# The bonus of a RWKV-7 head in two fp32r products in place of one fp32 product

## The chip, the cores and the metric

One Trainium2 chip, one of its cores. The metric is the time of one execution of the whole kernel on the device, in microseconds (us), the median of three runs. Engines: PE (TensorE, matrix products), DVE (VectorE), ACT (ScalarE), POOL (GpSimd), SP (SyncE, which issues most of the DMAs). fp32r is a second four-byte type of PE's inputs; the kernel splits an fp32 value into its copy in fp32r, the high part, and what that leaves, the low part.

## The reference

One layer of a hybrid decoder for 1024 prompt tokens and 8 x 4 sample tokens. One projection feeds RWKV-7 time mixing (8 heads of 64) and, beside it, dilated window attention (3 groups of 4 heads of 128); both are gated, projected, merged, and normalised. The change touches one term of the time mixing, the bonus:

```python
def rwkv_mix(zs, z_gate, wkv0, w0, w_w2, a0, w_a2, k_k, k_a, r_k, lnx_g, lnx_b):
    ...
    S_fin, o = lax.scan(step, wkv0.astype(F32), xs)
    ...
    o = ((o - mu) * lax.rsqrt(var + GN_EPS)).reshape(B, T, R_WIDTH) * lnx_g.astype(F32) + lnx_b.astype(F32)
    bonus = (jnp.sum(r * k * r_k.astype(F32), -1, keepdims=True) * v).reshape(B, T, R_WIDTH)
    y = (o + bonus) * jax.nn.silu(z_gate.astype(F32))
```

The sum runs over the 64 values of a head, for each token.

## The kernel before, in words

The activations stand transposed in SBUF (columns on the 128 partitions, tokens along the free axis), split once into a high and a low part, both fp32r. A weight block comes in by DMA (`load_w`, L159 to L163: `wraw`), ACT copies its high part to fp32r (`whi`, L162), DVE subtracts it for the low part (`wlo`, L163), and `mm3` (L172) makes three fp32r products of each pair, high by high, low by high and high by low, over chunks of 352 tokens into the PSUM banks `pj`. These products fill most of PE's time.

The time mixing runs from some 30 to 620 us. It is cut into eight units: head pair j (0 to 3, two heads on 128 partitions) times half hf (0 or 1, 512 tokens). A unit goes through four generators. `unit` prepares: norms of the keys, decays (L330), the scaled operands `KR` and `BK` (L346 to L356), the product of r, k and r_k in `rk` (L358), the two halves of the products `AT` (PE L370, DVE's masked copy L377), then the bonus (L389: `rk` by the matrix of ones per head `bones`, a part of the constants `cst`; L390 multiplies by v), transposed values `W` (PE L397, ACT L400), transposed keys `BT` (PE L407, ACT L408). `inverse` solves the triangular systems on DVE (L441, L444), `scan` (L463 to L511) carries the state over the chunks, `norm` (L544 to L557) normalises and adds the bonus.

The generators are advanced by one planner that keeps a clock of costs: each `yield (cost, due)` adds its cost to the clock and says when the stream may go on; between them the planner puts pieces of the projection's products. What comes out is PE's order, which is fixed by hand (a manual schedule for PE alone); the order on the other engines is made by the framework's scheduler. The bonus announces its cost at L391, `yield (0.85, D_G)`.

Tiles with the tag "t" are 128x512 fp32 in a ring of six buffers; the tag "g" is two PSUM banks, "sc" two, "pj" four. After the time mixing come the sample rows, the attention of the heads, the two branch products and the output stage (L1378, fp32r products of 512 columns).

Of the kernel before, what the change touches and what calls it, by code (L numbers as in the profile page):

```python
# [11 lines left out]
F32 = mybir.dt.float32  # L12
F32R = mybir.dt.float32r
I32 = mybir.dt.int32
AF = mybir.ActivationFunctionType
ALU = mybir.AluOpType
AX = mybir.AxisListType

P = 128
# [12 lines left out]
D_PN, D_KR, D_AT, D_G, D_W, D_INV, D_UP = 0.65, 1.81, 7.0, 0.2, 2.09, 0.9, 14.4  # L32
# [51 lines left out]
def tile_layer(ctx: ExitStack, tc: tile.TileContext, A: dict, O: list):  # L84
    nc = tc.nc
    V, S, G, T, SP = nc.vector, nc.scalar, nc.gpsimd, nc.tensor, nc.sync
# [10 lines left out]
    def mk(pool, shape, tag, bufs=None, dt=F32):  # L97
        uid[0] += 1
        return pool.tile(list(shape), dt, tag=tag, name=f"{tag}_{uid[0]}", bufs=bufs)

    def ps(tag, cols=512, parts=P):
        pool = pspool if tag == "pj" else pp[0]
        return mk(pool, [parts, cols], tag, {"pj": PJ, "sc": 2, "g": 6 - PJ, "s": 1, "t": 2, "o": 1}[tag])
# [12 lines left out]
    rp = rw_stack.enter_context(tc.tile_pool(name="rp", bufs=1))  # L116
# [3 lines left out]
    bones, rmask = cst[:, 0:128], cst[:, 384:896]  # L120
# [117 lines left out]
    V.tensor_scalar(der[:, HB : HB + 24], prm[:, BG : BG + 24], 0.5, None, ALU.mult)  # L238
    V.tensor_scalar(der[:, KA2 : KA2 + 4], prm[:, KA : KA + 4], -0.5, 1.0, ALU.mult, ALU.add)
    V.tensor_scalar(der[:, KAH : KAH + 4], prm[:, KA : KA + 4], 0.5, None, ALU.mult)  # L240
    lhi = mk(rp, [P, 512], "lhi", dt=F32R)
    llo = mk(rp, [P, 512], "llo", dt=F32R)
    S.activation(lhi[:], lraw, AF.Copy)
# [61 lines left out]
    def unit(j, hf, Mr, Mk, Mv, st, out):  # L305
# [50 lines left out]
        V.tensor_tensor(BK[:, :, 0:4:3, :], c2p(k2), c2p(Ei), ALU.mult)  # L356
        rk = t_()
        V.scalar_tensor_tensor(rk[:], Mr[:, sl], prm[:, RK + j : RK + j + 1], k2[:], ALU.mult, ALU.mult)  # L358
        done["prep"] += 1
        yield (0.45, D_AT)  # L360

# [2 lines left out]
        for h in range(2):  # L364
            pA = [ps("g") for e in range(2)]
            for q in range(4):
                c = 4 * h + q
                for e in range(2):
# [5 lines left out]
                        start=True, stop=True,  # L374
# [11 lines left out]
            yield None  # L386
        bon = t_("bon", 2)
        pb = ps("g")
        T.matmul(pb[:], bones, rk[:], start=True, stop=True)  # L389
        V.tensor_tensor(bon[:], pb[:], Mv[:, sl], ALU.mult)  # L390
        yield (0.85, D_G)  # L391


        W = mk(rp, [P, 8, P], "W", 2)
# [17 lines left out]
        for c2 in range(4):  # L412
            for e in range(2):
                for p in range(2):
# [3 lines left out]
                        start=True, stop=True,  # L418
# [244 lines left out]
    def units():  # L663
        for u in range(8):
            j, hf = u // 2, u % 2
            while j not in pairs:
                yield None
            M, st = pairs[j]
            yield from unit(j, hf, M[0], M[1], M[2], st, ready)
            done["unit"] += 1  # L670
        yield from sample_rows()
# [688 lines left out]
    for i in range(8):  # L1360
# [9 lines left out]
        for c, (c0, c1) in enumerate(zip(parts, parts[1:])):  # L1370
            cs = slice(c0, c1)
            pb = ps("pj", c1 - c0)
# [51 lines left out]
```

## Time and profile before

| | |
|---|---|
| median of three runs | 1381.0 us (1380.83 to 1381.04) |
| profiled execution | 1381.54 us |
| its span | 1379.8 us |
| mean granted clock of PE | 0.996 |
| PE busy | 1344.1 us, 97% |
| DVE busy | 804.0 us, 58% |
| ACT busy | 467.2 us, 34% |
| POOL busy | 67.2 us, 5% |

The profile is one execution as the hardware recorded it. Busy times are shares of the whole span; an engine that waits is idle, and the wait is put down to what released it. The ends of matrix products are modelled, so the time that PE spends on one is best read from the start of one to the start of the next.

### The profile page before, as it was taken

The page shows a single profiled execution, that of the slowest core. Times are in us where ns is not written, and L with a number is a line of the kernel's source. Part 1 is how long each engine was busy: PE and PEld are TensorE (multiplying, and loading weights), DVE is VectorE, ACT ScalarE, POOL GpSimd, SP SyncE. Part 2 cuts the span into 40 slices and gives each one's busy share as a digit, 9 for nine tenths or more (in the row PEclk, how much of TensorE's full clock was granted, in tenths as well). Part 3 has the DMA queues.
Part 4 walks back from the last instruction along what each step waited for, and adds up shares of the span by engine and source line. Part 5 has one row for each costly group of instructions (what it writes and reads, how often), then busy time and mean ns, then how long its engine had stood idle before and what let it go on. Part 6 is the DMA issues. An engine that isn't in the chain of part 4 may idle for free.

```text
span 1379.8 us, 25342 instructions
## 1 busy us (share of the span) xinstructions
PE 1344.1 (97%) x9809; PEld 1245.0 (90%) x9809; DVE 804.0 (58%) x2203; ACT 467.2 (34%) x1089; POOL 67.2 (5%) x82
## 2 busy tenths in 40 slices
PE   7999999999999999999999999999999999899997
PEld 7998998898988889999999999999999998799786
DVE  4358767677867757441555275437542845665565
ACT  4333434444344444431332333233323234132211
POOL 0000000000000000000100000000000000015100
PEclk9999999999999999999999999999999999999999
DMA  6112222412322242336645355635554556795221
GB/s 216 55 47 73 58 82 72 110 37 75 88 59 75 74 110 79 91 94 123 136 106 132 84 141 115 131 93 140 114 123 115 133 122 153 230 287 170 82 103 68
DMA packets 340270, 151.62 MB, mean 110 GB/s; under 512 B 188928, under 2 KB 329622, under 8 KB 339894
## 3 DMA queue, kind: packets, MB, share of 16 engines
q1 hardware_dynamic: 241270, 129.68, 34.6%
q10 hardware_dynamic: 98880, 20.32, 7.4%
q8 instruction: 77, 1.26, 0.4%
q14 instruction: 43, 0.35, 0.1%
HBM read 110.68 MB, written 38.97 MB: 108 GB/s over the span
## 4 chain that ended last, share of the span: by engine, by line
PE 74%; DVE 14%; DMA 7%; issue 2%; ACT 2%; SPq 1%; DVEq 0%; ACTq 0%
PE pj L172 52%; PE pj L1378 7%; DVE tm L441 2%; DVE X L444 2%; PE o L932 2%; DMA cb<-cd 2%; PE s L895 2%; DMA wraw<-in_w_in_dram 1%; DVE wlo L163 1%; DVE o L1178 1%; PE t L915 1%; PE sc L503 1%; PE s L1014 1%; PE g L370 1%; DVE AT L377 1%
## 5 line engine op out<-in xcount | busy, mean ns | idle before, releaser
L172 PE MATMUL pj<-xhi,whi 128*128 128x352 f32 x1848 | 398.7, 337 | 5.0 <-ACT xhi L1245 3.0
L172 PE MATMUL pj<-xlo,whi 128*128 128x352 f32 x1848 | 382.8, 328 | 0.0
L172 PE MATMUL pj<-xhi,wlo 128*128 128x352 f32 x1848 | 381.9, 328 | 0.4 <-DVE wlo L163 0.4
L172 PEld LDWEIGHTS pj<-xhi,whi 128*128 128x128 f32 x1848 | 302.9, 189 | 21.7 <-issue 10.5
L172 PEld LDWEIGHTS pj<-xhi,wlo 128*128 128x128 f32 x1848 | 307.6, 189 | 3.6 <-issue 1.2
L172 PEld LDWEIGHTS pj<-xlo,whi 128*128 128x128 f32 x1848 | 307.9, 189 | 2.5 <-issue 0.4
L163 DVE TENSOR_TENSOR wlo<-wraw,whi 128x512 fp32r<-128x512 f32 x162 | 113.4, 701 | 84.0 <-ACT whi L162 83.3
L162 ACT ACTIVATE whi<-wraw 128x512 fp32r<-128x512 f32 x162 | 100.6, 625 | 146.6 <-PE pj L172 89.0
L905 ACT ACTIVATE Sm<-Sm,nm 128x128 f32<-128x128 f32 (+1 forms) x96 | 42.4, 442 | 102.7 <-DVE nm L902 102.7
L511 DVE SCALAR_TENSOR_TENSOR st<-sc,E,SD 64x64 f32<-64x64 f32 x128 | 36.2, 283 | 47.7 <-PE sc L508 46.2
L441 DVE TENSOR_TENSOR tm<-Y,X 128x60 f32<-128x60 f32 (+24 forms) x248 | 52.6, 212 | 6.3
L444 DVE TENSOR_TENSOR X<-X,tm 128x60 f32<-128x60 f32 (+24 forms) x248 | 52.0, 210 | 6.4
L1378 PE MATMUL pj<-wl,mh 128*128 128x512 f32 (+1 forms) x136 | 52.0, 382 | 0.0
L897 DVE CUSTOM_DVE_ANT_0 Sm<-s,cst 128x128 f32<-128x128 f32 (+1 forms) x96 | 29.2, 346 | 39.0 <-PE s L895 38.3
L494 ACT ACTIVATE SD<-st,E 128x128 f32<-128x128 f32 x64 | 25.6, 400 | 58.5 <-DVE st L511 58.5
L758 POOL TENSOR_TENSOR kvp<-vv,kv 128x512 f32<-128x512 f32 x16 | 19.7, 1233 | 514.3 <-DVE Ss L766 387.0
L932 PE MATMUL o<-PT,Vt 128*128 128x128 f32 x280 | 38.7, 276 | 0.8 <-ACT PT L919 0.8
L895 PE MATMUL s<-k,q 128*128 128x128 f32 (+1 forms) x192 | 37.8, 326 | 1.7 <-DVE ml L897 1.6
L820 ACT ACTIVATE k<-pj 128x352 f32<-128x352 f32 (+1 forms) x36 | 16.2, 454 | 67.5 <-PE pj L172 60.9
L932 PEld LDWEIGHTS o<-PT,Vt 128*128 128x128 f32 x280 | 36.4, 191 | 1.5 <-ACT PT L919 1.1
L503 PEld LDWEIGHTS sc<-R,AT 64*64 64x64 f32 x256 | 19.7, 134 | 18.4 <-DVE R L498 7.9
L299 ACT ACTIVATE zt<-pj,der 128x352 f32<-128x352 f32 x48 | 26.4, 551 | 27.9 <-PE pj L172 26.7
(314 smaller groups left out, 1719.1 us busy)
## 6 DMA issues: line engine op xcount, KB each, us to landing
wraw<-in_w_in_dram SPq DMA_DIRECT2D x146, 256.0 KB
gd<-zt SPq DMA_DIRECT2D x48, 176.0 KB
gt<-gd SPq DMA_DIRECT2D x48, 176.0 KB
vs<-bt ACTq DMA_DIRECT2D x48, 128.0 KB
kc<-in_cache_kv_g_dram SPq DMA_DIRECT2D x48, 128.0 KB
Vt<-vs ACTq DMA_DIRECT2D x12, 512.0 KB
cb<-cd SPq DMA_DIRECT2D x12, 512.0 KB
zd<-zt SPq DMA_DIRECT2D x24, 176.0 KB
```

Of the source, the lines that this page charges most:

```text
L162: S.activation(hi[:], raw[:], AF.Copy)
L163: V.tensor_tensor(lo[:], raw[:], hi.bitcast(F32)[:], ALU.subtract)
L172: T.matmul(out, w[wi][:, n % 4, :], x[:, n % 4, :], start=first and n == 0, stop=last and n == 11)
L441: V.tensor_tensor(tm, Y[:, r : r + 1, r + 1 : 32].to_broadcast([P, m, n]), X[:, 0:m, r : r + 1].to_broadcast([P, m, n]), ALU.mult)
L444: V.tensor_tensor(X[:, 0:m, r + 1 : 32], X[:, 0:m, r + 1 : 32], tm, ALU.subtract)
L503: T.matmul(pu[u, 64 * e : 64 * e + 64], AT[u, e, c, u], R[u, 64 * e : 64 * e + 64], start=True, stop=True)
L511: V.scalar_tensor_tensor(S1[d, d], pS[d, d], E[d, c, 64:65], SD[d, d], ALU.mult, ALU.add)
L895: T.matmul(r, qT[:, i * P : (i + 1) * P], kT[:, keys[i][0] * P : keys[i][0] * P + n], start=True, stop=True)
L897: V.tensor_tensor_reduce(out=Sm[:, i, 0:n], in0=r, in1=m3 if g == 2 else m12[:, 256 - n : 256], scale=1.0, scalar=NEG, op0=ALU.add, op1=AL ...
L905: S.activation(Sm[:, i, 0:n], Sm[:, i, 0:n], AF.Exp, scale=SCALE, bias=nm[:, x : x + 1], accum_out=ml[:, g, 1, i : i + 1])
L932: T.matmul(po[:, (i % 4) * P : (i % 4 + 1) * P], st["Vt"][:, kb_, :], PT[:, n * P : (n + 1) * P], start=m == 0, stop=m == len(keys[i]) - 1,)
L1378: T.matmul(pb[:], a[:, k], wk, start=x == 0, stop=x == len(prods) - 1)
```

## The change

Three places. After the derived parameters, the matrix of ones is copied once into a fp32r tile, `bones_r`. In `unit`, behind `rk`, ACT copies `rk` to fp32r (`rkh`) and POOL subtracts that from `rk` (`rkl`, fp32r too); both come from the ring "t". The bonus then is two fp32r products that add up in the same bank, and it announces a cost of 0.47 in place of 0.85.

```diff
     V.tensor_scalar(der[:, KAH : KAH + 4], prm[:, KA : KA + 4], 0.5, None, ALU.mult)
+    bones_r = mk(rp, [P, P], "bones_r", dt=F32R)
+    V.tensor_copy(bones_r[:], bones)
     lhi = mk(rp, [P, 512], "lhi", dt=F32R)
...
         rk = t_()
         V.scalar_tensor_tensor(rk[:], Mr[:, sl], prm[:, RK + j : RK + j + 1], k2[:], ALU.mult, ALU.mult)
+        rkh, rkl = (mk(rp, [P, 512], "t", 6, dt=F32R) for _ in range(2))
+        S.activation(rkh[:], rk[:], AF.Copy)
+        G.tensor_tensor(rkl[:], rk[:], rkh.bitcast(F32)[:], ALU.subtract)
         done["prep"] += 1
         yield (0.45, D_AT)
...
         pb = ps("g")
-        T.matmul(pb[:], bones, rk[:], start=True, stop=True)
+        T.matmul(pb[:], bones_r[:], rkh[:], start=True, stop=False)
+        T.matmul(pb[:], bones_r[:], rkl[:], start=False, stop=True)
         V.tensor_tensor(bon[:], pb[:], Mv[:, sl], ALU.mult)
-        yield (0.85, D_G)
+        yield (0.47, D_G)
```

PE's order around the bonus of unit 4, before (L389 is the bonus, L172 the weight products, L496, L503 and L508 steps of the scan):

```order
L548 MATMUL g_3985<-ident_69,Ot_3216 128x128 x4
L389 MATMUL g_3997<-t_3842,cst_76 128x512
L496 MATMUL sc_4003<-st_114_794,KR_3043 128x128
L397 MATMUL g_4009<-ident_69,m_3442 128x128 x4
L172 MATMUL pj_3887<-xlo_9_87,whi_3891 128x352 x4
L503 MATMUL sc_4020<-R_4005,AT_3131 64x64 x2
L407 MATMUL g_4025<-ident_69,BK_3839 128x128 x4
```

And with the change (t_3866 is the high part, t_3867 the low one; line numbers from there on are higher by 2 to 7):

```order
L554 MATMUL g_4011<-ident_69,Ot_3238 128x128 x4
L394 MATMUL g_4023<-t_3866,bones_r_358 128x512
L395 MATMUL g_4023<-t_3867,bones_r_358 128x512
L502 MATMUL sc_4030<-st_115_796,KR_3060 128x128
L403 MATMUL g_4036<-ident_69,m_3464 128x128 x4
L172 MATMUL pj_3913<-xlo_9_87,whi_3917 128x352 x4
L509 MATMUL sc_4047<-R_4032,AT_3152 64x64 x2
L413 MATMUL g_4052<-ident_69,BK_3861 128x128 x4
```

The pair stands where the one product stood, here as in the units 0 to 5; what the planner puts behind the bonus changes only from unit 6 on.

ACT's order at the same place, before (L550 is the scaled copy of `norm`, L400 the copies of the transposed values, L499 the scan's output):

```order
L483 ACTIVATE AT_3131<-sc_3966 32x8x32 x2
L550 ACTIVATE Ot_3216<-g_3985,prm_339 128x512
L400 ACTIVATE W_4008<-g_4009 64x4x128
L499 ACTIVATE Ot_4000<-sc_4003 64x128
L400 ACTIVATE W_4008<-g_4009 64x4x128
L504 ACTIVATE W_3224<-sc_4020 64x128
```

With the change:

```order
L489 ACTIVATE AT_3152<-sc_3992 32x8x32 x2
L556 ACTIVATE Ot_3238<-g_4011,prm_339 128x512
L505 ACTIVATE Ot_4027<-sc_4030 64x128
L406 ACTIVATE W_4035<-g_4036 64x4x128 x2
L510 ACTIVATE W_3246<-sc_4047 64x128
```

The copy of the scan's output has moved ahead of the first of the two copies of the values.

DVE's order ahead of the masked copies of unit 7, before (L152 to L154 are the Newton steps of `norm`'s inverse root, L544 its scaling, L358 makes `rk`):

```order
L358 SCALAR_TENSOR_TENSOR t_6174<-m_4637,prm_339,t_6169 128x512
L152 SCALAR_TENSOR_TENSOR nt_6122<-nt_6122,v_1195_6119 128x8
L153 TENSOR_TENSOR nt_6122<-nt_6122 128x8
L154 SCALAR_TENSOR_TENSOR nt_6122<-nt_6122 128x8
L544 TENSOR_TENSOR Ot_5536<-Ot_5536,nt_6122 128x512
L377 TENSOR_TENSOR AT_6236<-g_6237,cst_76 128x512
```

With the change:

```order
L360 SCALAR_TENSOR_TENSOR t_6215<-m_4668,prm_339,t_6210 128x512
L152 SCALAR_TENSOR_TENSOR nt_6163<-nt_6163,v_1210_6160 128x8
L153 TENSOR_TENSOR nt_6163<-nt_6163 128x8
L154 SCALAR_TENSOR_TENSOR nt_6163<-nt_6163 128x8
L550 TENSOR_TENSOR Ot_5572<-Ot_5572,nt_6163 128x512
L163 TENSOR_TENSOR wlo_6683<-wraw_6680,whi_6682 128x512
L382 TENSOR_TENSOR AT_6284<-g_6285,cst_76 128x512
```

A subtraction of a weight split has come in ahead of the first masked copy.

## Rows read from the trace of the kernel before

**Rows 1.** The page: busy time, share of the span and instructions of PE.

```profile
PE 1344.1 (97%) x9809; PEld 1245.0 (90%) x9809; DVE 804.0 (58%) x2203; ACT 467.2 (34%) x1089; POOL 67.2 (5%) x82
```

**Rows 2.** Stretches: us, busy PE, PEld, DVE, ACT, POOL, clock, DMA share, GB/s.

```profile
30.00:620.00 590.00, 579.10 (x4659) 535.39 (x4658) 388.38 (x1311) 237.59 (x537) 6.88 (x20) 1.00 0.27 76
119.90:123.80 3.90, 2.87 (x26) 2.24 (x25) 3.66 (x15) 0.62 (x2) 0.00 (x0) 1.00 0.60 172
303.00:306.40 3.40, 3.40 (x14) 2.90 (x14) 3.30 (x16) 1.81 (x4) 0.00 (x0) 0.50 0.42 100
```

**Rows 3.** PE's waits from 30 to 640 us: total us, times, longest.

```profile
PE g L370 <- DVE AT L377: 2.7, 8, 1.0
PE g L407 <- ACT W L400: 2.6, 6, 0.4
```

**Rows 4.** Timeline of PE at unit 2's bonus: start, duration in us.

```profile
206.56 1.12 PE L389 MATMUL g<-t,cst 128*128 128x512 f32 x2
207.52 0.27 PE L496 MATMUL sc<-st,KR 128*128 128x128 f32 x1
```

**Rows 5.** Timeline of PE in the output stage, fp32r products of 512 columns.

```profile
1303.99 0.47 PE L1378 MATMUL pj<-xhi,mh 128*128 128x512 f32 x1
1304.30 0.39 PE L1378 MATMUL pj<-xhi,ml 128*128 128x512 f32 x1
1304.54 0.40 PE L1378 MATMUL pj<-wl,mh 128*128 128x512 f32 x1
```

**Rows 6.** The page's groups: ACT's copy to fp32r (busy us, mean ns).

```profile
L162 ACT ACTIVATE whi<-wraw 128x512 fp32r<-128x512 f32 x162 | 100.6, 625 | 146.6 <-PE pj L172 89.0
```

**Rows 7.** POOL's instructions of line 758: shortest, median, longest ns.

```profile
L758 POOL TENSOR_TENSOR kvp<-vv,kv x16: 1042/1044/1550, 656.0 to 1061.6; 128x512 f32<-128x512 f32 x16
```

**Rows 8.** Timelines of DVE and PE in unit 7: `rk` and its bonus.

```profile
499.03 0.74 DVE L358 SCALAR_TENSOR_TENSOR t<-m,prm,t 128x512 f32<-128x512 f32 x1
505.38 0.70 PE L389 MATMUL g<-t,cst 128*128 128x512 f32 x1
```

**Rows 9.** Timeline of DVE at the start; in brackets idle time and its releaser.

```profile
28.21 0.27 DVE L232 COPY shT<-g 128x104 f32<-128x104 f32 x1 [2.23 <-PE g L231]
```

**Rows 10.** Timelines of POOL and DVE in a later stage.

```profile
821.70 1.42 POOL L758 TENSOR_TENSOR kvp<-vv,kv 128x512 f32<-128x512 f32 x1 [30.74 <-DVE Ss L766]
822.14 1.53 DVE L767 TENSOR_TENSOR rtm<-Ss,kv 128x512 f32<-128x512 f32 x1
863.23 0.69 DVE L767 TENSOR_TENSOR rtm<-Ss,kv 128x512 f32<-128x512 f32 x1
```

**Rows 11.** Timelines of DVE and PE in unit 1.

```profile
119.97 0.69 DVE L163 TENSOR_TENSOR wlo<-wraw,whi 128x512 fp32r<-128x512 f32 x1
123.08 0.68 DVE L377 TENSOR_TENSOR AT<-g,cst 128x512 f32<-128x512 f32 x1
123.82 0.37 PE L370 MATMUL g<-KR,BK 64*128 64x128 f32 x1 [1.05 <-DVE AT L377]
```

**Rows 12.** Timelines of DVE and PE in unit 4.

```profile
320.83 0.15 DVE L154 SCALAR_TENSOR_TENSOR nt<-nt 128x8 f32<-128x8 f32 x1
322.12 0.44 DVE L463 STREAM_TRANSPOSE T<-AT 32x256 f32<-32x256 f32 x1
322.62 0.24 PE L467 MATMUL sc<-T,AT 32*32 32x32 f32 x2 [0.28 <-DVE T L463]
```

**Rows 13.** Timeline of DVE in units 2 and 3.

```profile
202.88 0.69 DVE L377 TENSOR_TENSOR AT<-g,cst 128x512 f32<-128x512 f32 x1 [0.79 <-PE g L370]
261.29 0.69 DVE L163 TENSOR_TENSOR wlo<-wraw,whi 128x512 fp32r<-128x512 f32 x1 [0.91 <-ACT whi L162]
```

**Rows 14.** Timelines of DVE and PE in units 6 and 7.

```profile
442.33 0.69 DVE L377 TENSOR_TENSOR AT<-g,cst 128x512 f32<-128x512 f32 x1 [0.53 <-PE g L370]
443.08 0.37 PE L370 MATMUL g<-KR,BK 64*128 64x128 f32 x1 [0.15 <-DVE AT L377]
502.46 0.37 PE L370 MATMUL g<-KR,BK 64*128 64x128 f32 x1 [0.15 <-DVE AT L377]
```

## The prediction

> **What bounds the kernel now.** I read the page first, then the stretch in which the change lies, then PE's waits there, then single instructions. The page gives PE busy for 97% of the span [rows 1]. The eight units (head pair 0 to 3 times half 0 or 1; I number them 0 to 7) run between 30 and 620 us, and there PE is busy for 579.10 of 590.00 us while DVE is busy for 388.38, ACT for 237.59 and POOL for 6.88 [rows 2]. So some 11 us of idle time is all that PE has there: time taken off PE is time off the span, unless PE then waits for something, and time that another engine loses costs nothing until PE waits for it. The places where PE waits are therefore the ones to read: the first products of a unit's second half (L370) wait 2.7 us in eight times, up to 1.0, for DVE's masked copy L377, and L407 waits 2.6 us in six for ACT's L400 [rows 3]. The first is where the change can hurt, since its new POOL instruction is put just ahead of it.
>
> One bound for the whole text: what a measurement of this kernel can tell from no change is about 0.2%, 2.76 us.
>
> **The product of the bonus (removed and added).** The fp32 product of 512 columns is two MATMULs; in unit 2 it starts at 206.56 and the next product starts at 207.52 [rows 4], so it holds PE for 0.96 us. For two fp32r products of 512 columns the nearest rows are those of the output stage: one starts at 1303.99 behind another kind of product, the next at 1304.30, the one behind both at 1304.54 [rows 5]. That is 0.55 us for two, the first dearer than the second (0.31 and 0.24); if both cost the second's, 0.48. The other end is that the pair is no cheaper than what it replaces, 0.96. I take 0.55, for the bonus too follows another kind of product. Saved: 0.96 - 0.55 = 0.41 a unit, **8 x 0.41 = 3.3 us** (ends: 0, and 8 x 0.48 = 3.8).
>
> The Trainium skill (TensorE: Matmul & The Clock Gate, section "Back-to-back issue gap") gives a lone product of N columns at full clock N/2.4 + 2.5 ns, 216 ns for 512 columns. By it the pair is an estimated 0.43 us, the saving 4.2 us and the sum below 0.9 us lower; the trace's 0.24 is a tenth above it, and the sum stays with the rows.
>
> What follows the bonus on PE starts sooner by 0.41. Behind it L407 waits 0.43 for ACT in six units [rows 3]; were that wait to grow by what PE gained, 6 x 0.41 = 2.5 of the 3.3 would go. I take it as kept: the order on ACT now has the copy of the scan's output ahead of both copies L400 in the middle units, where it stood between them, and so the second L400 starts sooner. Both ends (0 and 2.5) go to the range.
>
> **The high part on ACT (added).** Eight copies 128x512 to fp32r; the same form takes 625 ns [rows 6]. 8 x 0.63 = 5.0 us on an engine that idles 352 of the 590 us [rows 2]. I cost it at nothing; what hides it is that idle time, and if it stood in the way of the next unit's weight split on ACT, that would be late by 0.63 at most.
>
> **The low part on POOL (added), by itself.** A subtraction of 128x512 on POOL takes 1.04 us when alone, and up to 1.55 [rows 7]. POOL is idle otherwise. Is the bonus late for it? In unit 7, the tightest, the instruction that makes its input starts at 499.03 and takes 0.74, and the bonus starts at 505.38 [rows 8]: 5.6 us for a chain of 0.63 + 1.04 to 1.55, which fits in all units. At nothing, then, as to its own result. The change's conversion of the matrix of ones is one DVE copy at the start, ahead of L232, where DVE stands idle for 2.23 us [rows 9]: nothing.
>
> **What the low part does to DVE.** This is the term that decides. In the later stage, where POOL runs the same form beside DVE, a DVE instruction with two operands in SBUF that starts 0.44 us after POOL's at 821.70 takes 1.53 us; the same line takes 0.69 where POOL is quiet [rows 10]. POOL's own took 1.42 against 1.04. 821.70 + 1.42 = 823.12, and 822.14 + 1.53 = 823.67: DVE's ends 0.55 us after POOL's, so it did next to nothing until POOL had finished. So the two engines exclude each other, and POOL's 1.04 us is taken out of DVE's time wherever DVE has instructions with two SBUF operands to run. The low part starts about 0.7 us after its input is made, just in the stretch before L377.
>
> How much of 1.04 reaches PE is read from each unit's stretch:
> - Unit 1: DVE is busy for 3.66 of the 3.90 us from 119.90 [rows 2], from a weight split at 119.97 on, without a gap, to L377 at 123.08, for which PE's L370 already waits 1.05 [rows 11]. Everything DVE loses there, PE loses: between 0.7 (one instruction there, of 0.5, has an operand in PSUM and can run on if it comes to stand beside POOL's) and 1.04; I take 0.87.
> - Unit 4: the delay falls between L154 at 320.83 and the transposition L463 at 322.12, for which PE's L467 already waits 0.28 [rows 12]: 1.0.
> - Units 2 and 3: ahead of what follows DVE idles 0.79 and 0.91 us [rows 13], which takes up most of 1.04; 0.25 and 0.13 are left on DVE, about 0.12 each reaches PE. Units 0 and 5 are like them, 0.1 each.
> - Unit 6: idle 0.53 before L377, and PE waits 0.15 behind it already [rows 14]: 1.04 - 0.53 = 0.5, I take 0.4.
> - Unit 7: PE waits 0.15 [rows 14] and DVE's order now has a weight split (about 0.69, the form of [rows 11]) ahead of L377, behind POOL's instruction: 0.65.
>
> Sum of the losses: 0.87 + 1.0 + 2 x 0.12 + 2 x 0.1 + 0.4 + 0.65 = **3.4 us** (ends: 0, if the delays all fall into idle time, and 8 x 1.04 = 8.3, if none does).
>
> **The order.** The lower cost that the bonus announces leaves PE's order as it is through unit 5; from unit 6 on one group of four weight products stands earlier, and the rest follows shifted by one group. Nothing waits for that but what is named at unit 7. At nothing.
>
> **The sum.** -3.3 + 3.4 = +0.1 us on the profiled execution's 1381.54 (span 1379.8 and 1.7 around it), 1381.6. The runs' median, 1381.0, is 0.54 below that execution, so the forecast is **1381.1 us**: no change that can be told.
>
> **The rivals.**
> 1. *The whole gain arrives.* DVE's instruction stands first and POOL waits, or the delays fall into idle time. For it: POOL's 1.42 against 1.04 shows POOL waiting too [rows 10], and in four of eight units DVE has idle time there. Against it: the DVE row with 1.53 stands right behind. Without any loss the time is 1381.1 - 3.4 = 1377.7. The Trainium skill (SBUF — State Buffer, section "Who interferes with whom") says that the pair of ports that DVE and GpSimd share is locked for a whole instruction, and that the order of issue decides which of them is blocked; by that rule each order occurs, and the trace agrees with its lock (1.53 against 0.69). Chance 0.18.
> 2. *Slower: the lock reaches PE in full.* POOL's instruction starts right ahead of the DVE work on which PE waits in nearly every unit, and the idle times of units 2 and 3 lie at the wrong side of it. It decides from a mean loss of (3.3 + 2.7) / 8 = 0.75 us a unit on; in full it is 8 x 1.04 - 3.3 = +5.0, 1386.1. For it: unit 1 and 4. Against it: the idle times [rows 13]. Chance 0.10.
> 3. *Clock.* From 303.00 to 306.40 PE was busy throughout and its clock was 0.50, half speed [rows 2]; such a stretch costs half of its 3.40, 1.7 us. Against it: at 123.82, behind an idle time of 1.05 us, the clock stayed at 1.00 [rows 2, 11]. If the longer waits of units 1 and 4 (about 2.0 and 1.3) bring such a stretch, one gives 1382.8, two give 1384.5. Chance 0.10, half of it for two.
> 4. *The change doesn't do what it says:* the pair holds PE as long as the fp32 product, and only the losses are left: 1381.0 + 3.4 = 1384.4. Chance 0.02, since [rows 5] show the pair's form.
>
> **How the numbers follow.** The forecast has 0.60 and lies within 0.2% by its own ends (the wait at L407 grown by 2.5 gives 1383.6; a pair at 0.48 gives 1380.6). Faster by over 0.2% (below 1378.24) is rival 1: 0.18. Slower (over 1383.76) is rival 2, rival 3 with two stretches and rival 4: 0.10 + 0.05 + 0.02 = 0.17. The rest, 0.60 + 0.05, is the same: 0.65. The range goes from rival 1's 1377.7 to two stretches' 1384.5 and leaves out rival 2 and rival 1's lower part.
>
> **What would show it right or wrong.** From the start of the first product of the bonus to the product behind the second: 0.55, right; 0.96, rival 4. Beside POOL's eight subtractions DVE instructions of over 1.2 us: right; none: rival 1. PE's waits at L370 (a later line number by then) up from 2.7 to about 5: right; unchanged: rival 1; over 8: rival 2. A stretch at clock 0.50 that is not there now: rival 3. The forecast is wrong if PE's waits for DVE don't grow, or if PE's gain is taken by the wait for ACT behind the bonus.

## The result, and the profile after

The changed kernel takes 1383.12 us (median of 20 runs, 1381.72 to 1385.62), the kernel before on the same chip 1380.02 us (20 runs): a ratio of 1.0026, 95% interval 1.0018 to 1.0034, 2.5 to 4.7 us more. That is slower, by about the 0.2% that can be told: the interval leaves out no change. The range held it; the likeliest case, no change, did not happen. That 1383.12 still lies inside the forecast's band of no change (up to 1383.76) is luck: the band stood on three runs at 1381.0, and on the 1380.02 of twenty it would end at 1382.78. Of all executions reported from here on, one each of e4, e5 and e8 took 1628.62 to 3348.72 us and is left out of every figure.

The execution profiled after took 1384.94 us, its span is 1383.2 (1379.8 before), its mean clock 0.993 (0.996 before). First the page of after, the row of engines that answers to [rows 1]:

```profile
PE 1344.6 (97%) x9809; PEld 1248.4 (90%) x9809; DVE 809.2 (59%) x2204; ACT 471.7 (34%) x1097; POOL 77.7 (6%) x90
```

Then busy time by stretch, with the columns of [rows 2]: the time mixing, and three stretches behind PE's longest waits.

```profile
30.00:620.00 590.00, 576.53 (x4636) 535.42 (x4637) 391.66 (x1307) 240.97 (x542) 17.07 (x28) 0.99 0.27 75
125.90:129.30 3.40, 3.34 (x18) 3.12 (x19) 2.98 (x11) 0.00 (x0) 0.00 (x0) 0.50 0.15 53
327.30:330.70 3.40, 3.40 (x41) 3.14 (x36) 1.26 (x3) 1.53 (x3) 0.00 (x0) 0.50 0.46 108
508.20:511.60 3.40, 3.40 (x23) 3.14 (x17) 1.47 (x4) 1.80 (x5) 0.00 (x0) 0.50 0.25 39
```

PE as a whole is as busy as before, although its work has become less: in the three stretches its clock stood at half, 1.2 of 2.4 GHz. Before there was one such stretch in the time mixing, at 303.00 [rows 2]; that one is gone. Outside of the time mixing each of the two profiles has one more near 1180 us and ends in one of about 5 us.

PE's waits from 30 to 640 us in after, which answer to [rows 3]:

```profile
PE g L375 <- DVE AT L382: 5.1, 7, 2.0
PE sc L473 <- DVE T L469: 1.6, 2, 1.4
PE g L413 <- ACT W L406: 1.3, 5, 0.3
```

The wait for the masked copies rose from 2.7 to 5.1, that for the transposition in the scan from 0.5 to 1.6, while the wait behind the bonus for ACT fell from 2.6 to 1.3.

PE's timeline at the bonus, in unit 2 and, in the stretch at half clock, in unit 4:

```profile
208.67 0.51 PE L394 MATMUL g<-t,bones_r 128*128 128x512 f32 x1
209.01 0.40 PE L395 MATMUL g<-t,bones_r 128*128 128x512 f32 x1
209.24 0.28 PE L502 MATMUL sc<-st,KR 128*128 128x128 f32 x1
...
328.74 0.78 PE L394 MATMUL g<-t,bones_r 128*128 128x512 f32 x1
329.31 0.63 PE L395 MATMUL g<-t,bones_r 128*128 128x512 f32 x1
329.74 0.41 PE L502 MATMUL sc<-st,KR 128*128 128x128 f32 x1
```

From the first product to the work behind the second it takes 0.57 us where the fp32 product took 0.96 [rows 4]. In unit 4 it takes 1.00: there the clock takes back all that the pair saved (unit 7, too, has its pair in a stretch at half clock, and 1.00).

Now the place of the loss. All eight subtractions on POOL (shortest, median and longest ns), timelines of POOL, DVE and PE in units 1 and 4, and PE's wait in unit 7:

```profile
L363 POOL TENSOR_TENSOR t<-t,t x8: 1272/1394/1889, 90.7 to 502.9; 128x512 fp32r<-128x512 f32 x8
...
120.49 1.89 POOL L363 TENSOR_TENSOR t<-t,t 128x512 fp32r<-128x512 f32 x1 [28.46 <-ACT t L362]
121.28 1.16 DVE L450 TENSOR_TENSOR X<-X,tm 128x48 f32<-128x48 f32 x1
125.23 0.37 PE L375 MATMUL g<-KR,BK 64*128 64x128 f32 x1 [1.99 <-DVE AT L382]
...
321.57 1.27 POOL L363 TENSOR_TENSOR t<-t,t 128x512 fp32r<-128x512 f32 x1 [12.29 <-ACT t L362]
321.56 1.29 DVE L262 SCALAR_TENSOR_TENSOR m<-lst,prm,m 128x1 f32<-128x1 f32 x1
324.36 0.21 PE L473 MATMUL sc<-T,AT 32*32 32x32 f32 x1 [1.36 <-DVE T L469]
...
505.97 0.37 PE L375 MATMUL g<-KR,BK 64*128 64x128 f32 x1 [1.02 <-DVE AT L382]
```

A DVE instruction of one column lasts 1.29 us, as long as POOL's beside it (0.21 for the same line in a quiet place, at 320.76). In unit 1 POOL first waits for DVE's weight split, then holds up a step of the inverse. PE's wait at the masked copies is 1.99 where it was 1.05 [rows 11], and 1.36 where it was 0.28 [rows 12]. Some 0.7 and 3 us behind these two waits the first two stretches at half clock begin; the third begins at 508.2, 2.2 us behind the wait of 1.02 in unit 7, which was 0.15 [rows 14].

### The profile page after: what moved, and what is told of

It is laid out like the page before. It is cut to its first block, busy times and chain, and to the rows that moved or that the text cites. A ratio compares the mean times of both kernels' runs of the same rounds, so it can differ in the third digit from the quotient of the medians.

```text
span 1383.2 us, 25368 instructions
## 1 busy us (share of the span) xinstructions
PE 1344.6 (97%) x9809; PEld 1248.4 (90%) x9809; DVE 809.2 (59%) x2204; ACT 471.7 (34%) x1097; POOL 77.7 (6%) x90
## 4 chain that ended last, share of the span: by engine, by line
PE 74%; DVE 15%; DMA 6%; ACT 2%; issue 2%; SPq 1%; DVEq 0%; ACTq 0%
PE pj L172 52%; PE pj L1384 7%; PE o L938 2%; PE s L901 2%; DVE tm L447 2%; DVE X L450 2%; DMA wraw<-in_w_in_dram 1%; DVE wlo L163 1%; DMA cb<-cd 1%; PE sc L509 1%; PE t L921 1%; PE s L1020 1%; PE sc L514 1%; DMA cd<-nE 1%; PE sc L502 1%
## 5 line engine op out<-in xcount | busy, mean ns | idle before, releaser
L172 PE MATMUL pj<-xhi,whi 128*128 128x352 f32 x1848 | 397.1, 336 | 5.1 <-ACT xhi L1251 3.0
L172 PE MATMUL pj<-xhi,wlo 128*128 128x352 f32 x1848 | 382.6, 328 | 0.2 <-DVE wlo L163 0.2
L172 PE MATMUL pj<-xlo,whi 128*128 128x352 f32 x1848 | 382.4, 328 | 0.0
L172 PEld LDWEIGHTS pj<-xhi,whi 128*128 128x128 f32 x1848 | 304.0, 189 | 21.8 <-issue 10.3
L172 PEld LDWEIGHTS pj<-xhi,wlo 128*128 128x128 f32 x1848 | 306.7, 189 | 3.6 <-issue 0.8
L172 PEld LDWEIGHTS pj<-xlo,whi 128*128 128x128 f32 x1848 | 307.3, 189 | 1.6 <-issue 0.4
L504 DVE TENSOR_TENSOR R<-sc,R 64x128 f32<-64x128 f32 x64 | 18.4, 288 | 34.9 <-PE sc L502 33.8
L505 ACT ACTIVATE Ot<-sc 64x128 f32<-64x128 f32 x64 | 17.4, 272 | 57.6 <-DVE R L504 56.9
```

What stands on the lines that cost most here:

```text
L172: T.matmul(out, w[wi][:, n % 4, :], x[:, n % 4, :], start=first and n == 0, stop=last and n == 11)
```

## The experiments

Theory A: POOL's subtraction locks DVE out, PE's waits for DVE grow, and the longer waits bring stretches at half clock. Theory B: the changed order of the work is to blame. Theory C: the pair is no cheaper. Later, D and E: the stretches come because the fp32 product is gone (D), or because of the added waits (E).

In the table "clock" is the mean over a kernel's executions, and "without the clock" the median of each execution's time less (1 - its clock) x 1380 us, the time that the clock took if PE was the bound throughout. It is a rough measure (the clock is given to three digits) for comparing kernels: e8, which has the work of before and longer waits, comes out 0.8 us below it, so differences of under 1 us say nothing. The kernel before has 81 executions beside these, in three sets with 1373.1, 1373.2 and 1373.5. The last column counts PE's waits of 0.8 us or more between 31 and 620 us in the kernel's one profile.

| kernel | ratio to before (95%) | clock | without the clock, us | waits of 0.8 or more |
|---|---|---|---|---|
| before | 1 | 0.9955 | 1373.4 | 1 |
| after | 1.0026 (1.0018 to 1.0034) | 0.9921 | 1373.0 | 3 |
| e1, no low part | 0.9998 (0.9986 to 1.0010) | 0.9933 | 1371.2 | 3 |
| e2, split made, fp32 product | 1.0047 (1.0030 to 1.0065) | 0.9928 | 1376.4 | 2 |
| e3, subtraction on DVE | 1.0021 (1.0009 to 1.0032) | 0.9932 | 1373.2 | 4 |
| e4, on DVE between the masked copies | 0.9997 (0.9983 to 1.0012) | 0.9935 | 1370.4 | 3 |
| e5, as e4, cost 0.85 | 0.9994 (0.9985 to 1.0003) | 0.9941 | 1370.9 | 2 |
| e6, after with cost 0.85 | 1.0027 (1.0018 to 1.0037) | 0.9920 | 1372.1 | 3 |
| e7, as e5, fp32 product | 1.0001 (0.9992 to 1.0010) | 0.9957 | 1374.1 | 1 |
| e8, before with cost 0.47 | 1.0008 (0.9999 to 1.0017) | 0.9943 | 1372.6 | 2 |
| e10, e5 again | 0.9994 (0.9985 to 1.0003) | 0.9947 | 1370.6 | 2 |
| e11, e7 again | 1.0000 (0.9989 to 1.0012) | 0.9955 | 1373.2 | 1 |

**e1, the pair without the low part.**

```diff
-        rkh, rkl = (mk(rp, [P, 512], "t", 6, dt=F32R) for _ in range(2))
+        rkh = mk(rp, [P, 512], "t", 6, dt=F32R)
...
-        G.tensor_tensor(rkl[:], rk[:], rkh.bitcast(F32)[:], ALU.subtract)
...
-        T.matmul(pb[:], bones_r[:], rkl[:], start=False, stop=True)
+        T.matmul(pb[:], bones_r[:], rkh[:], start=False, stop=True)
```

> POOL's subtraction is taken out; the second fp32r product takes the high part again, so that the sum leaves out the low part and counts the high part twice. PE's order is that of the change. Theory A (POOL's lock on DVE lengthens PE's waits for the masked copies, and the longer waits bring stretches at half clock): the waits at the first products of the second half are back at 2.7 us or below, at most one stretch at half clock between 30 and 620 us, and only the gain is left: 8 x 0.4 = 3.2 us under the kernel before, a ratio of about 0.998. Theory B (the changed order of the work on PE, ACT and DVE costs the time): as the change, about 1.0026 of before. Theory C (the fp32r pair is no cheaper): about as before, 1.000.

Measured: 0.9998. PE's waits in e1, the sum and those of units 1, 3 and 7, and last unit 3's in the kernel before:

```profile
PE g L374 <- DVE AT L381: 3.7, 7, 1.0
...
123.36 0.37 PE L374 MATMUL g<-KR,BK 64*128 64x128 f32 x1 [1.04 <-DVE AT L381]
...
263.43 0.37 PE L374 MATMUL g<-KR,BK 64*128 64x128 f32 x1 [0.80 <-DVE AT L381]
...
502.65 0.37 PE L374 MATMUL g<-KR,BK 64*128 64x128 f32 x1 [0.82 <-DVE AT L381]
...
262.63 0.37 PE L370 MATMUL g<-KR,BK 64*128 64x128 f32 x1 [0.33 <-DVE AT L377]
```

Without POOL unit 1's wait is back at 1.04, with PE's order that of the change. So POOL makes the wait there, and taking it away gives 0.9998 against 1.0026: B falls as the main cause. But the expected 0.998 is not there. Units 3 and 7 still wait longer than before (unit 3: 0.80 against 0.33; unit 7: 0.82 against 0.15 [rows 14]), and the profile has three stretches at half clock, at 125.6, 265.5 and 504.5, behind the waits of units 1, 3 and 7.

**e2, the losses alone.**

```diff
-        T.matmul(pb[:], bones_r[:], rkh[:], start=True, stop=False)
-        T.matmul(pb[:], bones_r[:], rkl[:], start=False, stop=True)
+        T.matmul(pb[:], bones, rk[:], start=True, stop=True)
...
-        yield (0.47, D_G)
+        yield (0.85, D_G)
```

> The high and the low part are made as in the change, but the bonus is the fp32 product of before with its cost of 0.85, so PE's order is that of before; the split's results are not used. Theory A: the losses without the gain: waits for the masked copies of about 5 us, two or three stretches at half clock, and a time 3 us above the change, a ratio to before of about 1.0045 (from 1.003). Theory B: as before, 1.000, since PE's order is that of before. Theory C: as the change, 1.0026.

Measured: 1.0047, as theory A had it. The waits in e2, and the stretch behind unit 4's:

```profile
PE g L375 <- DVE AT L382: 4.3, 7, 2.0
...
125.04 0.37 PE L375 MATMUL g<-KR,BK 64*128 64x128 f32 x1 [2.00 <-DVE AT L382]
...
323.87 0.21 PE L472 MATMUL sc<-T,AT 32*32 32x32 f32 x1 [1.36 <-DVE T L468]
...
325.70:332.50 6.80, 6.80 (x59) 5.48 (x58) 3.20 (x6) 1.71 (x5) 0.00 (x0) 0.50 0.24 53
```

PE's order and its fp32 product are those of before, and the waits of units 1 and 4 are those of after to 0.01 us. B falls with this run; C falls with the rows of the pair above (this interval begins at 1.0030, below the change's upper end of 1.0034). The clock, 0.9928 in six executions against 0.9955, fell with PE's work unchanged: added waits are enough to bring the stretches. The one stretch in this profile lasts 6.8 us, twice as long as those of after.

**e3, the subtraction on DVE at the same place.**

```diff
-        G.tensor_tensor(rkl[:], rk[:], rkh.bitcast(F32)[:], ALU.subtract)
+        V.tensor_tensor(rkl[:], rk[:], rkh.bitcast(F32)[:], ALU.subtract)
```

> The subtraction at the same place in the program on DVE in place of POOL: 0.69 us of DVE's own time instead of a lock of 1.3 us. Theory A: about half of the loss (0.69 of 1.3), so waits for the masked copies of 3.5 to 4.5 us, and a ratio to before of 0.999 to 1.001; with no stretch at half clock more than before it is below 1.000. Theory B: as the change, 1.0026, since PE's order is the same.

Measured: 1.0021, a miss: the waits for the masked copies fell to 3.4, about as expected, but the time hardly did. The timelines of DVE and PE in unit 4 of e3:

```profile
321.02 1.28 DVE L382 TENSOR_TENSOR AT<-g,cst 128x512 f32<-128x512 f32 x2
322.34 0.43 DVE L469 STREAM_TRANSPOSE T<-AT 32x256 f32<-32x256 f32 x1
...
322.83 0.24 PE L473 MATMUL sc<-T,AT 32*32 32x32 f32 x2 [2.07 <-DVE T L469]
```

The scheduler's order on DVE changed with the 0.69 us: two masked copies now stand ahead of the transposition for which PE waits, and 1.28 us of them make that wait 2.07. In the same profile the bonus of unit 1 waits 1.02 for DVE. In this run the price of the DVE instruction was not its duration but where the rest of the order went.

**e4, the subtraction between the masked copies.** The mask sets column 64 of this tile to zero, so adding it changes nothing but makes the instruction wait for the first pair of masked copies.

```diff
-        G.tensor_tensor(rkl[:], rk[:], rkh.bitcast(F32)[:], ALU.subtract)
...
+            if h == 0:
+                V.scalar_tensor_tensor(rkl[:], rk[:], AT[:, 1, 0, 64:65], rkh.bitcast(F32)[:], ALU.add, ALU.subtract)
             yield (1.7, D_G)
```

> The subtraction on DVE, made to depend on the masked copies of a unit's first half (it adds a column of AT that the mask sets to zero), so that it stands between the two pairs of masked copies, where DVE idles for 1.04 us in units 2 and 6 of the kernel before. Theory A: nothing is lost in six units, at most 0.7 us each in units 1 and 4, where DVE is busy: 2 to 3 us under the kernel before, a ratio of 0.998 to 0.9985, with waits for the masked copies at or under 3.5 us. Theory B: as the change, 1.0026.

Measured: 0.9997; faster than the change, but not 2 to 3 us below before. Units 3 and 7 wait 0.88 and 0.82 in it. **e5** takes the order out as well: e4 with the announced cost of before.

```diff
-        yield (0.47, D_G)
+        yield (0.85, D_G)
```

> The subtraction on DVE between the two pairs of masked copies, and the announced cost back at 0.85, so that PE's order is that of the kernel before but for the pair in place of the product. PE's wait in unit 7 (0.82 with the cost of 0.47) should fall to about 0.15, that in unit 3 stay at 0.8 (it comes from the high part standing ahead of a weight split on ACT) or fall to 0.33 (it comes from the order). Theory E (the stretches at half clock come from the added waits): the mean granted clock is back near that of before (0.995), and the time is 2.5 to 3.2 us under the kernel before, a ratio of 0.9977 to 0.9982. Theory D (they come because the fp32 product, solid work for PE, is gone): the clock stays near 0.9935 and the ratio at 0.999 to 0.9997.

Measured: 0.9994, with a clock of 0.9941: the ratio is the one that theory D had forecast, not E's. DVE's timeline in unit 2 of e5, then PE's waits, and unit 3 on PE, ACT and SP; last ACT and SP there in the kernel before:

```profile
203.60 0.75 DVE L388 SCALAR_TENSOR_TENSOR t<-t,AT,t 128x512 fp32r<-128x512 f32 x1
204.52 1.29 DVE L381 TENSOR_TENSOR AT<-g,cst 128x512 f32<-128x512 f32 x2 [0.18 <-PE g L374]
...
PE g L374 <- DVE AT L381: 3.5, 8, 1.1
...
262.60 0.37 PE L374 MATMUL g<-KR,BK 64*128 64x128 f32 x1 [1.06 <-DVE AT L381]
...
260.15 0.55 ACT L301 ACTIVATE zt<-pj,der 128x352 f32<-128x352 f32 x1 [1.02 <-DMA gd<-zt]
260.60 0.62 ACT L162 ACTIVATE whi<-wraw 128x512 fp32r<-128x512 f32 x1
...
256.13 0.45 SPq L302 DMA_DIRECT2D gd<-zt  x1
...
260.18 0.55 ACT L299 ACTIVATE zt<-pj,der 128x352 f32<-128x352 f32 x1 [0.97 <-DMA gd<-zt]
...
256.90 0.45 SPq L300 DMA_DIRECT2D gd<-zt  x1
```

The subtraction lies in DVE's idle time and costs nothing. Unit 7's wait is gone, so it was the order's. Unit 3's is not: ACT waits there for a DMA that writes the gates (a ring of two buffers), and behind it stand the weight split on ACT, its subtraction on DVE, the masked copies, and PE. By then the pair has brought PE forward by 0.77 us (its products for the first half of unit 3 start at 259.75, before at 260.52). The write is issued 0.77 earlier too, but lets ACT go on at the same time as before, 4.0 us behind its issue where it was 3.3, and PE waits for it instead. Why the write takes longer, no run shows.

**e6, the change with the order of before.** Its only edit on the change is the line of the cost, 0.85 for 0.47.

> The change with the announced cost back at 0.85: PE's order is that of the kernel before but for the pair; POOL's subtraction stays where it was. Theory A (lock of DVE by POOL): the waits for the masked copies fall by unit 7's 0.7 alone, and the ratio to before is 1.0015 to 1.0025. Theory B (the order costs the time): 0.998.

Measured: 1.0027, no better than the change (A had 1.0015 to 1.0025), with a clock of 0.9920. Unit 7's wait is gone, unit 3's is now 1.17. B is out.

**e7, as e5 with the fp32 product.** Its edit on e5 is that of e2's first part.

> As the kernel with the subtraction between the masked copies and a cost of 0.85, but the bonus is the fp32 product of before; the split's results are not used. It differs from that kernel by the product alone: the time between the two is what the pair gains on PE, 8 x 0.4 = 3.2 us. Theory E: the same clock in both and 3.2 us between them; against before 1.000 to 1.0005. Theory D: the clock here is that of before (0.995), lower by 0.0015 in the kernel with the pair, and only 0.5 to 1.5 us between them.

Measured: 1.0001, and in **e11**, the same kernel again, 1.0000; e5 again, **e10**, 0.9994.

> The kernel with the subtraction between the masked copies and the cost of 0.85 once more, for a narrower interval and a second trace. Theory E and D both: a ratio of 0.9985 to 1.0003 as in the first; a wait in unit 3 of 0.8 to 1.1 us if it comes from the write of the gates, which the earlier products reach before it has landed, in every execution.

> The kernel with the split between the masked copies and the fp32 product once more. Between it and the one with the pair: 0.5 to 2.0 us in the median if half or more of the pair's 3.2 us is given back in waits and in stretches at half clock; 3 us if the first comparison was chance. Clock 0.0005 to 0.0015 above that of the pair if the stretches are part of it.

The two kernels differ by the product alone. In the medians the pair gives 1379.66 - 1379.12 = 0.5 and 1378.93 - 1378.20 = 0.7 us; without the clock it gives 3.2 and 2.6, about the 8 x 0.39 = 3.1 that its rows say. The clock is 0.0016 and 0.0008 lower with the pair, as D had it for e7; only the first of the two is clear of the scatter of the executions. Unit 3 on PE in e7 and the gates' write there:

```profile
262.80 0.37 PE L374 MATMUL g<-KR,BK 64*128 64x128 f32 x1 [0.35 <-DVE AT L381]
...
260.35 0.55 ACT L301 ACTIVATE zt<-pj,der 128x352 f32<-128x352 f32 x1 [0.28 <-DMA gd<-zt]
```

0.35 there against 1.06 in e5 and 0.86 in e10, and both profiles with the pair have a stretch at half clock right behind that wait (6.8 us from 263.9, 3.4 from 264.7), neither of those with the fp32 product. So the numbers came out as D had them, but the longer wait can explain them as well.

**e8, the order alone:** the kernel before with `yield (0.47, D_G)` in place of `yield (0.85, D_G)`.

> The kernel before with the announced cost of 0.47 in place of 0.85, nothing else: the order alone. Theory A: the wait in unit 7 goes from 0.15 to 0.8, nothing else changes, a ratio of 1.0005 (0.7 us). Theory B: 1.0026. Theory E: the clock is a little lower than before's; theory D: the clock is that of before.

Measured: 1.0008 (interval just at 1). Unit 7's wait is 0.82 in it, and unit 3's 0.69. The clock, 0.9943, is lower than before's with the fp32 product in place, as E has it.

**e9, POOL writes but reads nothing.**

```diff
-        rkh, rkl = (mk(rp, [P, 512], "t", 6, dt=F32R) for _ in range(2))
+        rkh, rkl = mk(rp, [P, 512], "t", 6, dt=F32R), mk(rp, [P, 512], "t", 6)
...
-        G.tensor_tensor(rkl[:], rk[:], rkh.bitcast(F32)[:], ALU.subtract)
+        G.memset(rkl[:], 0.0)
...
-        T.matmul(pb[:], bones_r[:], rkl[:], start=False, stop=True)
+        T.matmul(pb[:], bones_r[:], rkh[:], start=False, stop=True)
```

> POOL's subtraction is replaced by a POOL instruction that fills the same tile with zeros, reading nothing; the second product takes the high part again, so the low part is left out of the sum. If POOL's reading is what locks DVE out, no DVE instruction beside the eight POOL instructions lasts more than 0.1 us longer than elsewhere, and the wait in unit 1 is 1.05 us, as without POOL; if any POOL instruction on a large tile locks it, the wait in unit 1 is up to 2.0 and DVE instructions of over 1 us with operands of a few columns stand beside it.

Its one execution took 1376.68 us, too few for a ratio. The timeline of DVE and POOL at one of the eight places, and PE in unit 1:

```profile
117.28 0.69 DVE L355 TENSOR_TENSOR t<-m,t 128x512 f32<-128x512 f32 x1
...
117.30 0.53 POOL L363 MEMSET t<- 128x512 f32 x1 [28.62 <-DVE BK L357]
...
123.96 0.37 PE L375 MATMUL g<-KR,BK 64*128 64x128 f32 x1 [1.14 <-DVE AT L382]
```

DVE's two-operand instruction runs at its usual 0.69 beside POOL's; at all eight places those of 128x512 take 0.67 to 0.69. Unit 1's wait is 1.14. A POOL instruction that only writes does not hold DVE up; it is POOL's reading that locks DVE out. (The Trainium skill, SBUF — State Buffer, section "Who interferes with whom", says just this of two-operand DVE instructions and GpSimd instructions that read, and the runs agree on both sides of it.)

## Why the prediction was right and wrong

**The pair on PE.** Forecast 0.55 for two; measured, at full clock, 0.57 to 0.58 in units 2, 3, 5 and 6, and 0.53 and 0.48 in units 0 and 1, where it stands behind weight products, fp32r like itself. In unit 2 that saves 0.39, not 0.41. The rows of the output stage were the right ones.

**POOL's price.** Forecast 1.04 us from L758, which the prediction calls a subtraction; it is a multiplication of two operands that are repeated along an axis, with an fp32 output. The change's subtraction, with an fp32r output, took 1.27 at the shortest; which of the differences makes it dearer, no run shows. The mechanism was as told: in units 0, 1, 2, 4 and 6 a DVE instruction beside it took 1.15 to 1.66 us. In units 3 and 7 DVE's stood first, POOL took 1.48, and DVE lost nothing.

**The high part on ACT,** costed at nothing, was that: e7 and e11 make the whole split and stand at 1.0001 and 1.0000.

**What reaches PE.** Added waits for DVE by unit, after less before: 0.28, 0.94, 0.10, 0.21, 1.08, 0.13, none, 0.87, in sum 3.6. Forecast were 0.1, 0.87, 0.12, 0.12, 1.0, 0.1, 0.4, 0.65, in sum 3.4. Unit 4 and unit 1 make over half of it, as read from [rows 11, 12]. In unit 6 DVE's scaling took 1.66 us for 0.69, and PE lost almost nothing: half of that went into DVE's idle time ahead of the masked copies, and PE had a step of the scan to do meanwhile. e2 has the sum by itself: without the clock 1376.4 - 1373.4 = 3.0 us.

**The wait behind the bonus.** I took L407's wait as kept and bounded it by a loss of 2.5; it fell by 1.3 us, a small gain that I had not put into the sum. All of PE's listed waits from 31 to 640 us together rose by 2.7 us, from 9.6 to 12.3.

**The sum.** Without the clock the change is worth 1373.0 - 1373.4 = -0.4 us; forecast was +0.1, and the measure can't tell the two apart. So the terms were right as far as it shows, and the forecast of no change was wrong all the same.

**The step that failed** is the chance of the third rival. I gave 0.10 to added stretches at half clock and 0.05 to two of them, by the one wait of 1.05 us in the profile that left the clock at 1.00. (The stretch that the prediction cites for this ends at 123.80, before the wait does; but the trace does have 1.00 behind it, as the first line below shows.) In the profile after there are three in the time mixing for one before, two more, at the rival's price of 1.7 us each: 3.4 us, which is the difference of the spans, 1383.2 - 1379.8. Over all executions the clock falls from 0.9955 to 0.9921, 0.0034 x 1380 = 4.7 us at most. One wait in one execution said nothing of how often such a wait brings a stretch: in e8, whose order up to there is that of the kernel before, a stretch begins at 125.0, behind the same wait in unit 1, 1.05 us. The same place in the kernel before, then the wait and the stretch in e8:

```profile
123.80:127.20 3.40, 2.86 (x21) 2.18 (x22) 3.24 (x11) 0.00 (x0) 0.00 (x0) 1.00 0.18 63
...
123.89 0.37 PE L370 MATMUL g<-KR,BK 64*128 64x128 f32 x1 [1.05 <-DVE AT L377]
...
125.00:128.40 3.40, 3.40 (x17) 2.79 (x16) 2.97 (x10) 0.00 (x0) 0.00 (x0) 0.50 0.15 53
```

The thirteen profiles have 18 such stretches in the time mixing (3.4 us long, three of them 6.8). Of these, 16 begin 0.4 to 3 us behind the end of a PE wait of 0.4 to 2.1 us; the two near 520 us in e7 and e8 do not. Of the 29 waits of 0.8 us or more, 14 are followed by one within 3 us, and after has three such waits where before has one. So each long wait has a chance of a stretch, and the added waits cost more than their length.

**The order,** costed at nothing but for unit 7, was that: 0.82 there in e1, e4 and e8, and 0.15 or less with the cost of before.

**What stays open.** That added waits bring stretches is shown by e2, with PE's work unchanged. Whether the pair brings some by itself (theory D) isn't settled: with it, e5 and e10 lose 0.0008 to 0.0016 of clock against e7 and e11, but they also have the longer wait in unit 3, which comes from a DMA. The table's last column speaks for the waits: kernels with one long wait lose nothing against before, those with two lose 1.1 to 3.7 us by the clock, those with three or four 2.8 to 4.8; and among those with two, the pair (e5, e10: 1.9 and 1.1) loses no more than the fp32 product (e2, e8: 3.7 and 1.7). But each count is of one profile, and no run has the pair without the wait. A third buffer for the gates, which might take that wait away, wasn't tried. The clock of an execution is not the time mixing's alone, either: the stretch near 1175 us lasts 6.8 us in five of the profiles (e5, e6, e7, e10, e11) and 3.4 in the others. And no version beats the kernel before: e5 and e10 are 0.3% faster than the change, and at 0.9994 (0.9985 to 1.0003) twice not clear of before.

## What to carry to other kernels

An elementwise instruction given to an idle POOL is not free when it reads SBUF: here it stopped DVE's two-operand instructions, one of a single column too, until it was done, so look at who waits for DVE right then, and put the instruction where DVE idles (a false dependence on the work ahead of the hole does it). Where PE paces the kernel, cost an added wait at more than its length: here PE's clock dropped to half behind 14 of 29 waits of 0.8 us or more. And where PE is made faster ahead of a transfer, ask whether the transfer comes forward too.

## What the runs showed of the hardware

A DVE instruction on a single column with two operands in SBUF took 1.29 us beside POOL's subtraction and 0.21 elsewhere; beside a POOL instruction that only writes, DVE's kept its 0.69. POOL's subtraction of 128x512 took 1.27 us with fp32r output; a multiplication of the same shape with fp32 output took 1.04 [rows 7]. The pair of products took 1.00 us at a clock of 0.50 and 0.57 at 1.00. What I had not expected most: in a stream in which PE is busy for 97% of the time, waits of 0.8 to 2.1 us are followed by stretches of 3.4 or 6.8 us at half clock in about half of the cases, often enough to take back the whole gain of a cheaper product.
